# The expert layer of a two-block network on one core: unsplit weight planes, pinned row work, gates with tokens innermost

## The chip, the cores and the metric

The kernel runs on one core of one Trainium2 chip, in one launch. The metric is the device time in microseconds (us). TensorE is PE in the profile, VectorE is DVE, ScalarE is ACT, GpSimd is POOL, and SP only issues transfers.

## The reference, cut to what matters

Two transformer blocks run over 256 tokens of width 1024 in float32. The change lies in the last layer of the first block, an expert layer. Each token picks 16 of 16,384 experts in each of 8 heads, 128 in all:

```
q  = (xc @ w_query);  sc = q . sub_keys            # scores of 2 x 128 keys per head
top 16 of each half -> 256 sums -> top 16          # experts, with softmax gates
u  = expert_down[experts];  vv = expert_up[experts]  # rows of 1024
act = gelu(x . u);  w = gates * act
out = sum over 128 picks of w * vv
```

The second block, the attention of the first and the final normalisation are not touched.

## The kernel before, in words

**Two ways through the experts.** The first 64 tokens (`NS`) are done by fetching: 64 indirect transfers bring 128 rows of `down_rows` each (one per partition, 4 KB a row), and 64 more bring rows of `peer_up`. Partitions 0 to 63 hold one half of a token's picks, partitions 64 to 127 the other half. `fetch` (L733) issues one on the POOL queue into a ring of four buffers (`fetched`, L598); `dot` (L739) multiplies the rows with the token (`rows`, L602 to L604) and sums, one DVE instruction of 128x1024; `axpy` (L839) adds the weighted row of `peer_up` to `sums`, also one DVE instruction of 128x1024.

The other 192 tokens (`ND`) are done densely. **Stage 1** (L795 to L822) computes all 128 planes of 128 experts: a plane is a weight tile of 128x1024 float32, loaded by SP, and eight matmuls (one per slice of 128 columns) multiply it with the 192 tokens. Planes go in pairs, 64 pairs. The first of a pair is split: `stream` (L71) loads it, ACT casts it to a rounded part `hi` (L61), DVE makes the rest `lo` (L62), and `split_plane` (L776) multiplies `hi` with both parts of the tokens at once (384 columns) and `lo` with the rounded tokens (192 columns). The result is in two parts; ACT copies one (L811), DVE adds them (L812). The second plane of a pair is not split: `whole_plane` (L787) multiplies the float32 tile with float32 tokens `xf`. The trace shows such a float32 matmul as two records. ACT then takes the gelu of both planes into `slots` (L816), the SBUF array [128, 128 planes, 192 tokens].

**Gates.** `gates_of` (L745) builds the gates of four tokens as a one-hot matmul: four DVE instructions of 128x512, four ACT instructions, eight small matmuls into a PSUM bank (L767), and then the gates are multiplied into the planes that are finished (L772, DVE) and copied into the slots of those that are not (L774, ACT); a later plane finds its gate there, and DVE multiplies after the gelu (L818, L819). There are 48 such groups, spread between planes `J0` = 48 and `J1` = 120. L772 walks over planes innermost, so neighbouring elements in `slots` are 192 floats apart.

**Selection.** Ahead of stage 1, 16 query groups (L621 to L637) give the scores; DVE then finds the top lists of both halves of the tokens (L648 to L728), in part while stage 1 already runs, in memory that belongs to high planes of `slots`.

**Stage 2** (L862 to L882) runs over 128 `j`: `peer_up[j]` is split as above (L61, L62), the 192 columns of `slots[:, j]` are split into `a2` (L875 on ACT, L876 and L877 on DVE), and ten matmuls of 512 columns accumulate into four PSUM banks.

**Order.** A planner orders each engine's instructions by its own estimate of when each is ready, so the position in the code is a priority and not a place. `tc.keep_in_program_order` puts an instruction behind the one written just before it on its engine. In the kernel before, `dot` and `axpy` are free to move; the code places the dots between pairs 16 and 60 and the axpys over 112 of the 128 `j`. Each engine works in its own order. PSUM has four banks `mm` for planes and two banks `at` for gates.

Of the kernel before, what the change touches and what calls it, by code (L numbers as in the profile page):

```python
# [40 lines left out]
def layers_kernel(ctx: ExitStack, tc: tile.TileContext, a: dict, out: bass.AP, upto: str = "all"):  # L41
# [518 lines left out]
    with ExitStack() as c2:  # L560
        pr = c2.enter_context(tc.tile_pool(name="peer", bufs=1))
        prs = c2.enter_context(tc.tile_pool(name="peers", bufs=2))
        xhl = fx.tile([P, KT, 2, T], F32R, name="fhl")
# [181 lines left out]
        def gates_of(g, j):  # L745
# [27 lines left out]
            if j < P:
                S.copy(sv[:, :, j:], gv[:, :, j:])  # L774

        def split_plane(o, w):  # L776

            for k in range(KT):
                hi, lo = w[0][:, k * P:(k + 1) * P], w[1][:, k * P:(k + 1) * P]
                o2 = o[:, :2 * ND].rearrange("p (s t) -> p s t", s=2)  # L780
                if k < KT - 1:
                    PE.matmul(o2, hi, xhl[:, k, :, NS:], start=(k == 0), stop=False)  # L782
                PE.matmul(o[:, :ND], lo, xhl[:, k, 0, NS:], start=False, stop=False)  # L783
                if k == KT - 1:
                    PE.matmul(o2, hi, xhl[:, k, :, NS:], start=False, stop=True)
# [49 lines left out]
        S.activation(acts, acts, AF.Gelu)  # L835
        V.tensor_tensor(acts, acts, gate_s, op=OP.mult)
        sums = pr.tile([P, D], F32, name="sums", tag="rows_s")

        def axpy(k):  # L839
            r = fetch("peer_up", k)  # L840
            if k == 0:
                V.tensor_scalar(sums, r, acts[:, 0:1], None, op0=OP.mult)
            else:
                V.scalar_tensor_tensor(sums, r, acts[:, k:k + 1], sums, op0=OP.mult, op1=OP.add)  # L844
# [15 lines left out]
        state["k"] = 0  # L860
        K1 = 112
        for j in range(P):  # L862
            while state["k"] < min(HALF, -(-HALF * (j + 2) // K1)):
                axpy(state["k"])
                state["k"] += 1
                if state["k"] == HALF:

                    other = fetched()
                    S.copy(other[:NS], sums[NS:])
                    V.tensor_tensor(x_sb[:NS, 0, :], x_sb[:NS, 0, :], sums[:NS], op=OP.add)  # L870
                    V.tensor_tensor(x_sb[:NS, 0, :], x_sb[:NS, 0, :], other[:NS], op=OP.add)
# [484 lines left out]
```

## Time and profile before

| what | us |
|---|---|
| median of 3 runs | 1521.5 (1518.92 to 1528.25) |
| the profiled execution | 1522.0, span 1520.2 |
| PE busy, share of span | 1425.7, 94% |
| DVE busy | 1098.0, 72% |
| ACT busy | 787.9, 52% |
| POOL busy | 275.6, 18% |

The span is what the profiler saw from the first to the last instruction. [...] The stretches named below are us from the start of the span: the query groups run to about 225, stage 1 from 225 to 632, stage 2 from 632 to about 968, and the second block follows.

### The profile page before, as it was taken

To read this page: it belongs to the slowest core of one execution; us is meant where nothing else is said; L and a number is where in the kernel's file an instruction comes from. 1 tells how busy PE (TensorE), PEld (TensorE's weight loads), DVE (VectorE), ACT (ScalarE), POOL (GpSimd) and SP (SyncE) were. 2 spreads that over 40 slices of the span, in tenths; PEclk is the share of its full clock that TensorE was granted. 3 is DMA by queue.
4 is the path that set the end of the run, shared out by engine and by line. 5 is a ranking of instruction groups with operands and counts; after the bars stand their busy time and mean duration, and the time that the engine had idled before them with its cause. 6 is when DMAs were issued, how large, how long until landed. Compare 5 with 4: busy or idle time off the path is not lost. (4 is left out here: it accounts for less than half of the span.)

```text
span 1520.2 us, 23927 instructions
## 1 busy us (share of the span) xinstructions
PE 1425.7 (94%) x8728; PEld 1261.6 (83%) x8728; DVE 1098.0 (72%) x2133; ACT 787.9 (52%) x1440; POOL 275.6 (18%) x223
## 2 busy tenths in 40 slices
PE   9999995989988889877999999899999999999998
PEld 7778895989988878755888788798799988899886
DVE  7976479987999999878766666646285555566653
ACT  6475453443665555333555555557444545565542
POOL 4711100054333334543000000012001110000000
PEclk9999997999999999989999999999999999999999
DMA  7444653699999888988777776744255664466653
GB/s 272 139 153 153 211 166 125 192 361 380 341 341 316 299 297 286 336 305 297 229 227 223 224 229 226 245 154 153 95 169 173 190 193 153 127 197 192 192 189 116
DMA packets 93702, 336.92 MB, mean 222 GB/s; under 512 B 10736, under 2 KB 12656, under 8 KB 92816
## 3 DMA queue, kind: packets, MB, share of 16 engines
q1 hardware_dynamic: 73376, 259.79, 51.8%
q0 software_dynamic: 19344, 73.41, 13.7%
q10 hardware_dynamic: 864, 2.19, 0.4%
q8 instruction: 69, 1.13, 0.3%
q14 instruction: 49, 0.40, 0.1%
HBM read 331.15 MB, written 4.19 MB: 221 GB/s over the span
## 5 line engine op out<-in xcount | busy, mean ns | idle before, releaser
L62 DVE TENSOR_TENSOR lo<-raw,hi 128x1024 fp32r<-128x1024 f32 x420 | 517.7, 1235 | 296.9 <-ACT hi L61 295.7
L61 ACT CAST hi<-raw 128x1024 fp32r<-128x1024 f32 x420 | 440.5, 1050 | 436.4 <-PE mm L89 115.1
L88 PE MATMUL mm<-rows_h,hi 128*128 128x256 f32 x736 | 204.2, 283 | 2.6 <-ACT qT_x L1194 1.1
L90 PE MATMUL mm<-rows_h,lo 128*128 128x256 f32 x736 | 204.7, 280 | 1.0 <-DVE lo L62 1.0
L89 PE MATMUL mm<-rows_l,hi 128*128 128x256 f32 x736 | 205.0, 280 | 0.0
L789 PE MATMUL mm<-ff,raw_w 128*128 128x192 f32 x1024 | 184.2, 334 | 11.7 <-DVE mm L812 5.0
L789 PEld LDWEIGHTS mm<-ff,raw_w 128*128 128x128 f32 x1024 | 171.3, 194 | 15.4 <-DVE mm L812 6.1
L782 PE MATMUL mm<-fhl,hi 128*128 128x384 f32 x448 | 142.7, 379 | 20.0 <-DVE mm L812 18.6
L88 PEld LDWEIGHTS mm<-rows_h,hi 128*128 128x128 f32 x736 | 137.4, 189 | 4.4 <-ACT hi L61 1.4
L90 PEld LDWEIGHTS mm<-rows_h,lo 128*128 128x128 f32 x736 | 138.6, 189 | 1.6 <-DVE lo L62 1.6
L89 PEld LDWEIGHTS mm<-rows_l,hi 128*128 128x128 f32 x736 | 138.7, 189 | 0.6
L783 PE MATMUL mm<-fhl,lo 128*128 128x192 f32 x512 | 120.6, 256 | 0.0
L735 POOL DMA_INDIRECT fetched<-in_down_rows,picks x64 | 78.2, 1222 | 230.4 <-DVE picks L713 119.9
L853 PE MATMUL mm<-hi,a 128*128 128x512 f32 x256 | 101.7, 405 | 15.8 <-ACT hi L61 7.5
L735 POOL DMA_INDIRECT fetched<-in_peer_up,picks x64 | 90.5, 1414 | 125.0 <-DVE sums L844 74.9
L854 PE MATMUL mm<-lo,a 128*128 128x512 f32 x256 | 101.5, 405 | 5.9 <-DVE lo L62 5.9
L782 PEld LDWEIGHTS mm<-fhl,hi 128*128 128x128 f32 x448 | 85.2, 190 | 22.6 <-issue 15.8
L857 PE MATMUL mm<-lo,a 128*128 128x512 f32 x256 | 102.6, 405 | 0.0
L856 PE MATMUL mm<-hi,a 128*128 128x512 f32 x256 | 100.0, 403 | 0.7 <-ACT a L875 0.7
L783 PEld LDWEIGHTS mm<-fhl,lo 128*128 128x128 f32 x512 | 97.4, 192 | 0.0
L844 DVE SCALAR_TENSOR_TENSOR sums<-fetched,acts,sums 128x1024 f32<-128x1024 f32 x63 | 81.4, 1292 | 10.9 <-DMA fetched<-in_peer_up,picks 10.8
L858 PE MATMUL mm<-hi,a 128*128 128x512 f32 x256 | 85.1, 405 | 0.0
(384 smaller groups left out, 2830.3 us busy)
## 6 DMA issues: line engine op xcount, KB each, us to landing
raw<-in_peer_up SPq DMA_DIRECT2D x128, 512.0 KB
raw_w<-in_peer_down SPq DMA_DIRECT2D x64, 512.0 KB
raw<-in_peer_down SPq DMA_DIRECT2D x64, 512.0 KB
raw<-in_w_in_2t SPq DMA_DIRECT2D x52, 512.0 KB
raw<-in_w_up SPq DMA_DIRECT2D x32, 512.0 KB
raw<-in_w_down SPq DMA_DIRECT2D x32, 512.0 KB
raw<-in_w_in SPq DMA_DIRECT2D x24, 512.0 KB
raw<-in_peer_query SPq DMA_DIRECT2D x16, 512.0 KB
```

The source lines that it names most:

```text
L61: S.copy(hi, src)
L62: V.tensor_tensor(lo, src, f32v(hi), op=OP.subtract)
L88: PE.matmul(o, hi, xh[:, k, :], start=(k == 0), stop=False)
L89: PE.matmul(o, hi, xl[:, k, :], start=False, stop=False)
L90: PE.matmul(o, lo, xh[:, k, :], start=False, stop=(k == kts - 1))
L735: G.indirect_dma_start(out=r, out_offset=None, in_=tables[table], in_offset=bass.IndirectOffsetOnAxis(ap=picks[:, k:k + 1], axis=0))
L782: PE.matmul(o2, hi, xhl[:, k, :, NS:], start=(k == 0), stop=False)
L783: PE.matmul(o[:, :ND], lo, xhl[:, k, 0, NS:], start=False, stop=False)
L789: PE.matmul(o, w[:, k * P:(k + 1) * P], xf[:, k, :], start=(k == 0), stop=(k == KT - 1))
L853: PE.matmul(acc[0][hf], a2[:, 0:P], uh[:, ds], start=first, stop=False)
L854: PE.matmul(acc[0][hf], a2[:, 0:P], ul[:, ds], start=False, stop=last)
L857: PE.matmul(acc[1][hf], a2[:, P:2 * P], ul[:, ds], start=False, stop=False)
```

## The change

Stage 1 loads every plane by the new `stream_whole` and multiplies it by `whole_plane`; `split_plane` and the joining of two parts go, and a pair needs one PSUM bank instead of two. `stream_whole` takes its buffers in turn from the three rings of `raw`, `hi` and `lo`, nine in all. `dot` and `axpy` are pinned in program order and become steps of one list of 128: 92 (`KD`) of them, all 64 dots and 28 axpys, are spread over pairs 12 to 63 of stage 1, the other 36 axpys over the first 112 `j` of stage 2. The ring of fetched rows has five buffers. The gates start at plane 34 and end at 122, and L772 and L774 walk with the four tokens of a group innermost, so that PSUM is read with steps of 128 floats and `slots` in runs of four. The load of the gain and the making of `rows` move from ahead of the query groups to behind them. In `a2` the two DVE subtractions become one of 192 columns and ACT gets a second copy of 64.

```
--- before.py
+++ after.py
@@ -81,6 +81,16 @@
         with tc.high_priority():
             split(raw, hi, lo)
         return hi, lo
+    whole = {"at": 0}
+    def stream_whole(src):
+        tag = ("raw", "hi", "lo")[whole["at"] % 3]
+        whole["at"] += 1
+        w = stream_p.tile([P, CH], F32, name="whole", tag=tag, bufs=3)
+        nc.sync.dma_start(w, src)
+        return w
     def gemm_t(o, xh, xl, w, kts=KT):
         for k in range(kts):
...
@@ -595,13 +605,8 @@
 
         def fetched():
-            return pr.tile([P, D], F32, name="fetched", tag="fetched", bufs=4)
-        grow = fetched()
-        nc.scalar.dma_start(grow, bass.AP(tensor=a["ffn_gain"].tensor, offset=0, ap=[[0, P], [1, D]]))
-        rows = pr.tile([P, D], F32, name="rows_s", tag="rows_s")
-        V.scalar_tensor_tensor(rows[:NS], x_sb[:NS, 0, :], rs_peer[0][:NS], grow[:NS], op0=OP.mult, op1=OP.mult)
-        S.copy(rows[NS:], rows[:NS])
+            return pr.tile([P, D], F32, name="fetched", tag="fetched", bufs=5)
         picks = pr.tile([P, HALF], U32, name="picks")
         gate_s = pr.tile([P, HALF], F32, name="gate_s")
         acts = pr.tile([P, HALF], F32, name="acts")
@@ -636,6 +641,11 @@
             for t in range(NT):
                 S.copy(sc[t][:, hq * 4:hq * 4 + 4, :].rearrange("p a b -> p (a b)"), pss[t])
+        grow = fetched()
+        nc.scalar.dma_start(grow, bass.AP(tensor=a["ffn_gain"].tensor, offset=0, ap=[[0, P], [1, D]]))
+        rows = pr.tile([P, D], F32, name="rows_s", tag="rows_s")
+        V.scalar_tensor_tensor(rows[:NS], x_sb[:NS, 0, :], rs_peer[0][:NS], grow[:NS], op0=OP.mult, op1=OP.mult)
+        S.copy(rows[NS:], rows[:NS])
         tc.keep_in_program_order(V.tensor_copy(iota, iota_f[:, :, None].to_broadcast([P, P, 2])))
         BIG = -3.0e38
@@ -738,7 +748,36 @@
         def dot(k):
             r = fetch("down_rows", k)
-            V.scalar_tensor_tensor(r, r, 1.0, rows, op0=OP.mult, op1=OP.mult, accum_out=acts[:, k:k + 1])
+            tc.keep_in_program_order(V.scalar_tensor_tensor(r, r, 1.0, rows, op0=OP.mult, op1=OP.mult,
+                                                            accum_out=acts[:, k:k + 1]))
+        sums = pr.tile([P, D], F32, name="sums")
+        def axpy(k):
+            r = fetch("peer_up", k)
+            if k == 0:
+                d = V.tensor_scalar(sums, r, acts[:, 0:1], None, op0=OP.mult)
+            else:
+                d = V.scalar_tensor_tensor(sums, r, acts[:, k:k + 1], sums, op0=OP.mult, op1=OP.add)
+            tc.keep_in_program_order(d)
+            if k == HALF - 1:
+                other = fetched()
+                S.copy(other[:NS], sums[NS:])
+                V.tensor_tensor(x_sb[:NS, 0, :], x_sb[:NS, 0, :], sums[:NS], op=OP.add)
+                V.tensor_tensor(x_sb[:NS, 0, :], x_sb[:NS, 0, :], other[:NS], op=OP.add)
+        def step():
+            k = state["k"]
+            state["k"] += 1
+            if k < HALF:
+                dot(k)
+            else:
+                if k == HALF:
+                    S.activation(acts, acts, AF.Gelu)
+                    V.tensor_tensor(acts, acts, gate_s, op=OP.mult)
+                axpy(k - HALF)
         state = {"g": G0, "k": 0}
@@ -766,50 +805,33 @@
                 for i in range(2):
                     PE.matmul(ps[:, k * P:(k + 1) * P], oh1[:, k // 2, :, k % 2], og[i][:, k // 2, :, k % 2],
                               start=(i == 0), stop=(i == 1))
-            gv = ps.rearrange("p (t j) -> p t j", t=TG)
-            sv = slots[:, :, cs].rearrange("p j t -> p t j")
+            gv = ps.rearrange("p (t j) -> p j t", t=TG)
+            sv = slots[:, :, cs]
             if j > 0:
-                V.tensor_tensor(sv[:, :, :j], gv[:, :, :j], sv[:, :, :j], op=OP.mult)
+                V.tensor_tensor(sv[:, :j], gv[:, :j], sv[:, :j], op=OP.mult)
             if j < P:
-                S.copy(sv[:, :, j:], gv[:, :, j:])
-        def split_plane(o, w):
...
         def whole_plane(o, w):
             for k in range(KT):
                 PE.matmul(o, w[:, k * P:(k + 1) * P], xf[:, k, :], start=(k == 0), stop=(k == KT - 1))
-        J0 = 48
-        J1 = 120
-        K0 = 16
-        K1 = 60
+        J0 = 34
+        J1 = 122
+        K0 = 12
+        KD = 92
         for jp in range(P // 2):
             j = 2 * jp
             if j >= J0:
                 while state["g"] < min(NG, G0 - (-(NG - G0) * (j - J0 + 2) // (J1 - J0))):
                     gates_of(state["g"], j)
                     state["g"] += 1
-            while state["k"] < min(HALF, HALF * (jp - K0 + 1) // (K1 - K0)):
-                dot(state["k"])
-                state["k"] += 1
+            while state["k"] < KD * (jp - K0 + 1) // (P // 2 - K0):
+                step()
             nt = state["g"] * TG - NS
-            o1, o = mm_tile(), mm_tile()
-            split_plane(o1, stream(a["peer_down"][j]))
-            raw = pr.tile([P, CH], F32, name="raw_w", tag="raw_w", bufs=2)
-            nc.sync.dma_start(raw, a["peer_down"][j + 1])
-            whole_plane(o[:, ND:2 * ND], raw)
-            part = prs.tile([P, ND], F32, name="part", tag="og0")
-            S.copy(part, o1[:, ND:2 * ND])
-            V.tensor_tensor(o[:, :ND], o1[:, :ND], part, op=OP.add)
+            o = mm_tile()
+            for jj in range(2):
+                whole_plane(o[:, jj * ND:(jj + 1) * ND], stream_whole(a["peer_down"][j + jj]))
             ov = o[:, :2 * ND].rearrange("p (j t) -> p j t", j=2)
             dst = slots[:, j:j + 2, :]
             if nt < ND:
@@ -832,64 +854,46 @@
         acc = [[mm_tile() for _ in range(2)] for _ in range(NT)]
         held = []
...
         def ups(j, w, t):
             uh, ul, a2 = w
+            both, high, low = a2[:, ND:ND + P], a2[:, NS:ND], a2[:, T + NS:]
             first, last = (j == 0), (j == P - 1)
             for hf in range(2):
                 ds = slice(hf * 512, (hf + 1) * 512)
                 if t == 0:
-                    PE.matmul(acc[0][hf], a2[:, 0:P], uh[:, ds], start=first, stop=False)
-                    PE.matmul(acc[0][hf], a2[:, 0:P], ul[:, ds], start=False, stop=last)
+                    PE.matmul(acc[0][hf], both, uh[:, ds], start=first, stop=False)
+                    PE.matmul(acc[0][hf], both, ul[:, ds], start=False, stop=last)
                 else:
-                    PE.matmul(acc[1][hf], a2[:, P:2 * P], uh[:, ds], start=first, stop=False)
-                    PE.matmul(acc[1][hf], a2[:, P:2 * P], ul[:, ds], start=False, stop=False)
-                    PE.matmul(acc[1][hf], a2[:, 2 * P:], uh[:, ds], start=False, stop=last)
-        K1 = 112
+        KU = 112
         for j in range(P):
...
+            while state["k"] < min(2 * HALF, KD + -(-(2 * HALF - KD) * (j + 1) // KU)):
+                step()
             uh, ul = stream(a["peer_up"][j])
-            a2 = prs.tile([P, 6 * NS], F32R, name="a2", tag="oh1")
-            S.copy(a2[:, NS:4 * NS], slots[:, j, :])
-            V.tensor_tensor(a2[:, :NS], slots[:, j, :NS], f32v(a2[:, NS:2 * NS]), op=OP.subtract)
-            V.tensor_tensor(a2[:, 4 * NS:], slots[:, j, NS:], f32v(a2[:, 2 * NS:4 * NS]), op=OP.subtract)
+            a2 = prs.tile([P, 7 * NS], F32R, name="a2", tag="oh1")
+            S.copy(a2[:, :ND], slots[:, j, :])
+            S.copy(a2[:, ND:T], slots[:, j, :NS])
+            V.tensor_tensor(a2[:, T:], slots[:, j, :], f32v(a2[:, :ND]), op=OP.subtract)
...
```

## Rows read from the trace of the kernel before

**Rows 1.** Windows: start:end, length, PE, PEld, DVE, ACT, POOL busy, PEclk, DMA
```profile
225.00:240.00 15.00, 15.00 (x104) 15.00 (x103) 11.77 (x50) 8.10 (x13) 0.00 (x0) 1.00 0.57 182
240.00:270.00 30.00, 14.44 (x85) 14.17 (x84) 30.00 (x191) 7.14 (x13) 0.00 (x0) 0.72 0.27 90
270.00:300.00 30.00, 29.36 (x193) 29.04 (x193) 30.00 (x120) 10.45 (x18) 0.00 (x0) 1.00 0.65 206
300.00:345.00 45.00, 38.74 (x243) 37.10 (x243) 38.59 (x73) 20.74 (x45) 23.98 (x17) 0.98 0.96 354
345.00:372.00 27.00, 25.05 (x162) 24.82 (x161) 17.78 (x31) 8.79 (x15) 12.94 (x10) 0.96 0.98 367
372.00:470.00 98.00, 89.78 (x670) 86.66 (x667) 97.53 (x203) 62.02 (x159) 33.51 (x31) 1.00 0.95 342
470.00:570.00 100.00, 86.54 (x616) 81.32 (x616) 100.00 (x181) 58.61 (x157) 35.51 (x28) 0.98 0.88 303
570.00:632.00 62.00, 56.85 (x392) 54.39 (x392) 59.67 (x92) 28.75 (x75) 28.53 (x18) 0.97 0.85 295
632.00:720.00 88.00, 65.84 (x229) 48.25 (x230) 70.61 (x99) 30.39 (x46) 35.48 (x28) 0.86 0.87 316
720.00:920.00 200.00, 200.00 (x858) 160.60 (x857) 135.74 (x258) 112.90 (x172) 0.00 (x0) 1.00 0.72 226
```

**Rows 2.** Timeline of PE in stage 1: start, us, line, operation, count, [idle]
```profile
233.43 2.76 PE L789 MATMUL mm<-ff,raw_w 128*128 128x192 f32 x16
235.89 0.47 PE L782 MATMUL mm<-fhl,hi 128*128 128x384 f32 x1
238.30 2.76 PE L789 MATMUL mm<-ff,raw_w 128*128 128x192 f32 x16
...
457.56 0.63 PE L767 MATMUL at<-og,oh 128*128 128x128 f16 x8 [1.31 <-DVE oh L760]
458.03 2.81 PE L789 MATMUL mm<-ff,raw_w 128*128 128x192 f32 x16
```

**Rows 3.** Waits between 225 and 300: engine, line, releaser: total us, times, longest
```profile
PE mm L782 <- DVE mm L812: 16.2, 2, 15.6
```

**Rows 4.** Lines of DVE, 225 to 632: count, busy us, mean ns, idle
```profile
L62 DVE TENSOR_TENSOR lo<-raw,hi 128x1024 fp32r<-128x1024 f32 x65 | 81.3, 1251 | 8.1 <-ACT hi L61 8.1
L741 DVE SCALAR_TENSOR_TENSOR fetched<-fetched,rows_s 128x1024 f32<-128x1024 f32 x64 | 77.9, 1218 | 7.9 <-DMA fetched<-in_down_rows,picks 7.9
L844 DVE SCALAR_TENSOR_TENSOR sums<-fetched,acts,sums 128x1024 f32<-128x1024 f32 x35 | 45.4, 1298 | 2.3 <-DMA fetched<-in_peer_up,picks 2.3
L812 DVE TENSOR_TENSOR mm<-mm,part 128x192 f32<-128x192 f32 x63 | 24.6, 391 | 2.6 <-issue 2.6
```

**Rows 5.** Lines of DVE by shape, 372 to 632, PSUM times slots
```profile
L772 DVE TENSOR_TENSOR slots<-at,slots 128x456 f32<-128x456 f32 x2 | 2.4, 1218 | 0.0
L772 DVE TENSOR_TENSOR slots<-at,slots 128x192 f32<-128x192 f32 x2 | 1.1, 576 | 0.3 <-ACT slots L816 0.3
L819 DVE TENSOR_TENSOR slots<-mm,slots 128x384 f32<-128x384 f32 x3 | 1.7, 571 | 0.0
```

**Rows 6.** Timelines of DVE and PE in the query groups
```profile
173.44 1.28 DVE L603 SCALAR_TENSOR_TENSOR rows_s<-x_sb,rrow,fetched 64x1024 f32<-64x1024 f32 x1 [4.62 <-DMA fetched<-in_ffn_gain]
...
175.17 0.38 PE L89 MATMUL mm<-fhl,hi 128*128 128x256 f32 x1 [1.98 <-DVE fhl L188]
```

**Rows 7.** Lines of DVE, 632 to 720
```profile
L844 DVE SCALAR_TENSOR_TENSOR sums<-fetched,acts,sums 128x1024 f32<-128x1024 f32 x29 | 37.2, 1283 | 8.5 <-DMA fetched<-in_peer_up,picks 8.4
L62 DVE TENSOR_TENSOR lo<-raw,hi 128x1024 fp32r<-128x1024 f32 x22 | 25.9, 1222 | 4.8 <-ACT hi L61 4.7
```

**Rows 8.** Lines of DVE and ACT, 720 to 968
```profile
L877 DVE TENSOR_TENSOR a<-slots,a 128x128 fp32r<-128x128 f32 x104 | 29.6, 284 | 0.0
L876 DVE TENSOR_TENSOR a<-slots,a 128x64 fp32r<-128x64 f32 x104 | 22.7, 218 | 0.2 <-ACT a L875 0.2
...
L875 ACT CAST a<-slots 128x192 fp32r<-128x192 f32 x104 | 36.1, 347 | 3.3 <-PE mm L858 1.3 <-issue 1.0 <-ACT hi L61 1.0
```

More of the change, by code (lines that the diff above doesn't have):

```diff
@@ L562, in layers_kernel @@
         prs = c2.enter_context(tc.tile_pool(name="peers", bufs=2))
-        xhl = fx.tile([P, KT, 2, T], F32R, name="fhl")
-        xh, xl = xhl[:, :, 0, :], xhl[:, :, 1, :]
+        xh = fx.tile([P, KT, T], F32R, name="fh")
+        xl = fx.tile([P, KT, T], F32R, name="fl")
         xf = pr.tile([P, KT, ND], F32, name="ff")
@@ L768, in gates_of @@
                               start=(i == 0), stop=(i == 1))
-            gv = ps.rearrange("p (t j) -> p t j", t=TG)
-            sv = slots[:, :, cs].rearrange("p j t -> p t j")
+            gv = ps.rearrange("p (t j) -> p j t", t=TG)
+            sv = slots[:, :, cs]
             if j > 0:
-                V.tensor_tensor(sv[:, :, :j], gv[:, :, :j], sv[:, :, :j], op=OP.mult)
+                V.tensor_tensor(sv[:, :j], gv[:, :j], sv[:, :j], op=OP.mult)
             if j < P:
-                S.copy(sv[:, :, j:], gv[:, :, j:])
-        def split_plane(o, w):
[L778 to L785, printed above, removed]
+                S.copy(sv[:, j:], gv[:, j:])
         def whole_plane(o, w):
@@ L833, in layers_kernel @@
         held = []
[L835 to L844, printed above, removed]
         def ups(j, w, t):
             uh, ul, a2 = w
+            both, high, low = a2[:, ND:ND + P], a2[:, NS:ND], a2[:, T + NS:]
             first, last = (j == 0), (j == P - 1)
@@ L852, in ups @@
                 if t == 0:
-                    PE.matmul(acc[0][hf], a2[:, 0:P], uh[:, ds], start=first, stop=False)
-                    PE.matmul(acc[0][hf], a2[:, 0:P], ul[:, ds], start=False, stop=last)
-                else:
-                    PE.matmul(acc[1][hf], a2[:, P:2 * P], uh[:, ds], start=first, stop=False)
-                    PE.matmul(acc[1][hf], a2[:, P:2 * P], ul[:, ds], start=False, stop=False)
-                    PE.matmul(acc[1][hf], a2[:, 2 * P:], uh[:, ds], start=False, stop=last)
-        state["k"] = 0
-        K1 = 112
-        for j in range(P):
[L863 to L871, printed above, removed]
+                    PE.matmul(acc[0][hf], both, uh[:, ds], start=first, stop=False)
+                    PE.matmul(acc[0][hf], both, ul[:, ds], start=False, stop=last)
+                else:
+                    PE.matmul(acc[1][hf], high, uh[:, ds], start=first, stop=False)
+                    PE.matmul(acc[1][hf], high, ul[:, ds], start=False, stop=False)
+                    PE.matmul(acc[1][hf], low, uh[:, ds], start=False, stop=last)
+        KU = 112
+        for j in range(P):
+            while state["k"] < min(2 * HALF, KD + -(-(2 * HALF - KD) * (j + 1) // KU)):
+                step()
             uh, ul = stream(a["peer_up"][j])
-            a2 = prs.tile([P, 6 * NS], F32R, name="a2", tag="oh1")
-            S.copy(a2[:, NS:4 * NS], slots[:, j, :])
-            V.tensor_tensor(a2[:, :NS], slots[:, j, :NS], f32v(a2[:, NS:2 * NS]), op=OP.subtract)
-            V.tensor_tensor(a2[:, 4 * NS:], slots[:, j, NS:], f32v(a2[:, 2 * NS:4 * NS]), op=OP.subtract)
+            a2 = prs.tile([P, 7 * NS], F32R, name="a2", tag="oh1")
+            S.copy(a2[:, :ND], slots[:, j, :])
+            S.copy(a2[:, ND:T], slots[:, j, :NS])
+            V.tensor_tensor(a2[:, T:], slots[:, j, :], f32v(a2[:, :ND]), op=OP.subtract)
             if j >= P - LASTN:
@@ L882, in layers_kernel @@
                     ups(j, (uh, ul, a2), t)
-        lows = fetched()
+        moved = fetched()
         for t in range(NT):
@@ L889, in layers_kernel @@
                 if t == 0:
-                    S.copy(lows[NS:, ds], acc[0][hf][:NS])
+                    S.copy(moved[NS:, ds], acc[0][hf][:NS])
                     V.tensor_tensor(x_sb[NS:, 0, ds], acc[0][hf][NS:], x_sb[NS:, 0, ds], op=OP.add)
-                    V.tensor_tensor(x_sb[NS:, 0, ds], lows[NS:, ds], x_sb[NS:, 0, ds], op=OP.add)
+                    V.tensor_tensor(x_sb[NS:, 0, ds], moved[NS:, ds], x_sb[NS:, 0, ds], op=OP.add)
                 else:
```

## The prediction

> **What bounds the kernel now.** I read the windows by stretch first, because the change touches two stages only. In stage 1 (225 to 632) PE is never full for long, while DVE is: 30.00 of 30.00 us twice, then 97.53 of 98.00 and 100.00 of 100.00 [rows 1]. [...] So stage 1 is bound by DVE, first by the selection, later by the sum of splits, gates and row work. Stage 2 is two stages in one: from 632 to 720 PE is busy for 65.84 of 88.00 us and DMA moves 316 GB/s at a share of 0.87; from 720 on PE has 200.00 of 200.00 us [rows 1]. The lines of DVE say what is special in the first part: 29 of the 63 adding axpys, beside only 22 splits [rows 7]. The planner let them run as early as they could, although the code spreads them.
>
> **What PE needs.** The pitch comes from starts, not from busy time. A whole plane starts at 233.43 and the split plane behind it at 235.89: 2.46 us. That one takes until 238.30: 2.41 us. A gate group takes 458.03 - 457.56 = 0.47 us [rows 2]. Before, stage 1 needs of PE 64 x (2.46 + 2.41) + 48 x 0.47 = 334 us; it takes 632 - 225 = 407 [rows 1]. So 73 us are waits and low clock. After, it needs 128 x 2.46 + 48 x 0.47 = 337 us: **on PE itself the change costs 3 us**, and what it can gain is the 73.
>
> **What DVE loses and gets.** Its busy time in stage 1, summed over the eight windows, is 385 us [rows 1]. Out go the splits (65 records, 81.3 us) and L812 (63 records, 24.6 us). Row work was 64 dots and 34 adding axpys and the first axpy, some 99; 92 remain, 7 less of 1.3 us, 9 us [rows 4]. That leaves 385 - 81 - 25 - 9 = 270 us in a stage of at least 337. Up to pair 16 no gate exists, so DVE stands nowhere between PE and the gelu, and the 15.6 us stop has no cause left. ACT loses 64 casts and 64 copies and was not full (58.61 of 100 us) [rows 1].
>
> L772 walks differently. Its time rises from 576 ns for 192 elements to 1218 for 456, that is 2.4 ns an element, or 1.04 us at 384; L819, with PSUM and `slots` both in runs, takes 571 ns for 384 [rows 5]. The new walk has runs of four in `slots` but steps in PSUM. Bounds: 0.47 us less for each of 48 (23 us less on DVE) if the stride in `slots` was the price; as much more if the stride in PSUM costs the same. I take 0 on the path: 270 + 23 still lies under 337. [...]
>
> **What the transfers must carry.** A plane and a fetch are both 128x1024 float32 [rows 4], 0.524 MB. In pairs 17 to 63 (47 pairs) a pair brings two planes and 92/52 = 1.77 fetches, 1.976 MB, in the 2 x 2.46 + 48 x 0.47/47 = 5.40 us that PE needs: 366 GB/s. The windows give 354 at a share of 0.96, 367 at 0.98, 342 at 0.95, 303 at 0.88, 295 at 0.85 [rows 1]; scaled to a full share these are 344 to 374. So PE and DMA would be full at the same time. Lower bound of the loss: 0, at 374 (5.28 us a pair), with nine plane buffers and five fetch buffers to even it out. Upper bound: 300 to 372, where DMA was at 0.96 to 0.98, shows PE busy for 63.8 of 72 us [rows 1]; 11% of 47 x 5.40 = 254 us is 28 us. At 344 it is 5.74 us, 16 us in all. I take 15, near that. Stage 1 then takes 337 + 15 = 352: **55 us less**, between 42 and 70.
>
> [...]
>
> **Stage 2.** 858 matmuls in 200 us at ten a `j` are 2.33 us a `j`; the first 88 us hold 229, 22.9 `j`, worth 53.4 us at that pace [rows 1]. The bunched axpys thus cost 34.6 us, part of it low clock (0.86). After, 36 axpys are spread over 112 `j`. Per `j` DVE has 1.22 for the split, 0.32 x 1.28 = 0.41 for rows, and one subtraction of 192 in place of 0.284 + 0.218 (between those 0.50 and 0.28; I take 0.35): 1.98 of 2.33 us [rows 7, 8]. ACT has 112.90/200 of 2.33 = 1.32 and a copy of 64, at most the 0.347 of the copy of 192: 1.66 [rows 1, 8]. DMA carries 1.32 x 0.524 MB in 2.33 us, 297 GB/s, under 344. PE stays the bound. The pin puts each axpy on DVE behind the subtraction of the `j` before, which waits for one of two `a2` buffers, so it can't run ahead; queued behind a waiting axpy are the subtraction and the split of this `j`, and PE behind those with the other buffers still full. I subtract 5 us for that (0 to 15): **30 us less**, 20 to 35.
>
> **Rows made later.** L603 waits 4.62 us for the gain on DVE, with the query's transposes queued behind; PE stops for 1.98 us [rows 6]. Behind the query groups, the load (on ACT's queue), L603 (1.28 us) and ACT's copy fall where DVE feeds only the selection and PE has four banks. I take the 1.98: **2 us less**, 0 to 4.6.
>
> **Sum.** The profiled execution took 1522.0 (span 1520.2), the median is 1521.5: they agree. 1522 - 55 - 30 - 2 = **1435**; with all bounds good 1522 - 70 - 35 - 5 = 1412, with all bad 1522 - 42 - 20 - 0 = 1460. The second block is not touched.
>
> **Rivals.**
> - *Transfers never limit* (14 in 100): stage 1 at 337 to 340, 1412 to 1422. For it: 367 GB/s was seen. Against: PE waited beside it.
> - *Transfers become the bound* (13 in 100): fetches and planes together get what 470 to 632 shows, 299 GB/s: 6.61 us a pair, 47 x 1.21 = 57 us lost, stage 1 at 394, total 1522 - 13 - 30 - 2 = 1477. Against: DVE was full there and set the pace, and the DMA share was only 0.85 to 0.88.
> - *The pin doesn't spread the axpys in stage 2* (6 in 100), so the change doesn't do what it says: 36 in a bunch cost 36/29 x 34.6 = 43 us, 8 more than before: 1522 - 55 + 8 - 2 = 1473. Against it is the buffer wait named above.
> - *Slower* (5 in 100): a pinned row instruction waits for its fetch, and gates, multiplications and splits queue behind it on DVE, until the two gate banks and four plane banks are full. Measured waits for fetches are 7.9 + 2.3 + 8.5 = 18.7 us over 128 [rows 4, 7], 0.15 each, for instructions that the planner could move out of the way. Spare are 67 us of DVE in stage 1; with the 87 of the sum, it decides from (67 + 87)/128 = 1.2 us a row. At 1.6 us it would be 205 - 67 = 138 more: 1573. The fifth buffer and a pace of one per 3.1 us speak against it.
>
> **Chances.** The forecast as it stands has 62 in 100. The range 1412 to 1478 holds it, the first rival, and most of the next two; beyond it lies the slower one and worse mixtures, about 1 in 10. About 1%, 15 us, is what a measurement here can tell from no change. Faster by more than that: the first four cases, less a little for mixtures, 0.92; within 0.04; slower 0.04.
>
> **What would show it.** Right: the 240 to 270 stretch at a clock of 1.0; plane starts 2.46 us apart; stage 1 within 337 to 365 us, with DMA at a share over 0.9 and DVE near 270 us busy; axpys at even distances to the end of stage 2's first 112 `j`, and 2.33 to 2.4 us a `j`. Wrong: PE waiting for planes for over 30 us (transfers), DVE idle before row instructions for over 1 us each with PE idle beside it (pins), an L772 well above 1.2 us, or a clock below 0.95 in stage 1, which sixteen float32 matmuls in a row would then have caused.

## The result and the profile after

The changed kernel takes **1475.95 us** (median of four, 1475.67 to 1476.70) against 1522.38 for the kernel before beside it: a ratio of 0.9692 [0.9661, 0.9723]. That is 46 us faster, where 87 were forecast. The profiled span went from 1520.2 to 1474.4 us, 45.8 less. The stages are cut at the first matmul of each:

| us | before | after | forecast for after |
|---|---|---|---|
| up to stage 1 | 225.4 | 226.1 | 2 less |
| stage 1 | 406.7 | 362.6 | 352 |
| stage 2, to the start of its last `j` | 335.3 | 333.7 | 30 less |
| the rest | 552.8 | 552.0 | unchanged |

**Nearly all of the gain is stage 1's (44.1 us), and stage 2 gave 1.6.** The windows of the changed kernel, with the columns of [rows 1]:

```profile
225.00:240.00 15.00, 15.00 (x98) 15.00 (x97) 9.64 (x58) 3.71 (x6) 1.13 (x2) 1.00 1.02 390
240.00:270.00 30.00, 30.00 (x187) 30.00 (x186) 30.00 (x190) 6.30 (x11) 0.00 (x0) 1.00 0.65 214
270.00:300.00 30.00, 27.77 (x164) 27.41 (x163) 28.32 (x119) 8.83 (x23) 6.57 (x5) 0.94 0.65 228
300.00:345.00 45.00, 45.00 (x308) 44.68 (x307) 27.31 (x63) 13.99 (x45) 18.29 (x15) 1.00 0.99 370
345.00:372.00 27.00, 27.00 (x190) 26.68 (x189) 18.18 (x45) 9.19 (x31) 11.48 (x9) 1.00 0.96 353
372.00:420.00 48.00, 48.00 (x346) 47.42 (x344) 34.44 (x84) 20.24 (x68) 17.68 (x14) 1.00 0.95 346
420.00:470.00 50.00, 50.00 (x355) 49.42 (x355) 37.04 (x89) 18.28 (x63) 19.84 (x16) 1.00 0.94 335
470.00:520.00 50.00, 50.00 (x358) 49.42 (x356) 40.04 (x88) 19.57 (x69) 19.24 (x17) 1.00 0.96 346
520.00:570.00 50.00, 50.00 (x354) 49.42 (x353) 35.85 (x60) 15.94 (x59) 13.30 (x15) 1.00 0.95 353
570.00:592.00 22.00, 22.00 (x131) 21.42 (x131) 15.55 (x19) 4.85 (x7) 10.61 (x8) 1.00 0.74 258
592.00:640.00 48.00, 44.66 (x182) 32.67 (x181) 34.69 (x43) 26.39 (x55) 10.07 (x8) 1.00 0.83 286
640.00:720.00 80.00, 73.53 (x303) 55.02 (x302) 55.95 (x70) 43.22 (x91) 12.86 (x10) 1.00 0.81 262
720.00:800.00 80.00, 73.67 (x298) 55.70 (x299) 54.93 (x70) 42.23 (x90) 10.92 (x10) 0.98 0.81 263
800.00:880.00 80.00, 76.17 (x316) 57.61 (x315) 60.39 (x76) 47.06 (x97) 7.91 (x5) 1.00 0.73 238
880.00:923.00 43.00, 43.00 (x186) 34.48 (x185) 25.77 (x35) 25.05 (x50) 0.00 (x0) 1.00 0.72 229
```

In 240 to 270, where PE was busy for 14.44 us at a clock of 0.72 (0.50 in 250 to 260, where PE stood still), it now has 30.00 of 30.00 us at 1.00, although DVE is as full as before. What is left of the stop stands in 270 to 300, at a clock of 0.94: PE's transposes of the selected lists (L732) wait there for DVE's L709.

```profile
276.68 0.33 PE L732 MATMUL tp<-ident,slots 128*128 128x128 f32 x1 [2.23 <-DVE slots L709]
276.84 9.97 PE L817 MATMUL mm<-ff,whole 128*128 128x192 f32 x50
```

From 300 to the end of stage 1 at 588.7 PE is never idle, DVE has slack, and DMA works at a share of 0.94 to 0.99 until 570. DVE's busy time up to 592 sums to 276 us. In stage 2 the picture is the opposite of the one before: the first 88 us used to be poor and the rest full [rows 1], and now PE falls short evenly, 73.5 to 76 of 80 us, until the last adding axpy at 870.5; behind that it is full.

PE's timeline in stage 1 (start, us, engine, line, operation, tiles, shape, count; L817 is the whole plane, 16 records each, L806 a gate group):

```profile
424.18 5.42 PE L817 MATMUL mm<-ff,whole 128*128 128x192 f32 x32
429.43 0.62 PE L806 MATMUL at<-og,oh 128*128 128x128 f16 x8
429.89 5.42 PE L817 MATMUL mm<-ff,whole 128*128 128x192 f32 x32
435.15 0.62 PE L806 MATMUL at<-og,oh 128*128 128x128 f16 x8
```

Two planes take 429.43 - 424.18 = 5.25 us from start to start, 0.164 us a record; the forecast had 4.92. The same 5.25 stands at 332 (332.26 to 337.52) and at 545.

DVE's lines by shape from 372 on (count, busy us, mean ns, idle) show the gates' multiplication with its new walk, at L811:

```profile
L811 DVE TENSOR_TENSOR slots<-at,slots 128x456 f32<-128x456 f32 x1 | 0.6, 626 | 0.0
...
L811 DVE TENSOR_TENSOR slots<-at,slots 128x384 f32<-128x384 f32 x1 | 0.6, 551 | 0.0
```

456 elements took 1218 ns [rows 5] and take 626. All 48 together take 22.4 us, 467 ns in the mean.

Stage 2's waits, from 592 to 923 (engine, line, releaser: us in total, times, longest; L61 and L62 make `hi` and `lo`, L868 is a matmul, L879 the copy of 192 into `a2`, L761 the axpy):

```profile
POOL fetched L745 <- DVE sums L761: 197.3, 30, 10.7
DVE lo L62 <- ACT hi L61: 96.8, 92, 3.6
ACT hi L61 <- PE mm L870: 81.7, 78, 3.2
ACT hi L61 <- DMA raw<-in_peer_up: 61.3, 30, 3.7
PEld mm L868 <- ACT a L879: 24.7, 20, 2.3
PE mm L868 <- ACT a L879: 16.5, 14, 1.9
```

Thirty times ACT's cast stands still for a weight tile on its way, 61.3 us in all. One of these stops in the timeline (POOL's fetch, SP's weight loads, ACT, then PE; the row of SP groups three issues that begin at 653.22):

```profile
652.32 1.68 POOL L745 DMA_INDIRECT fetched<-in_peer_up,picks  x1 [7.94 <-DVE sums L761]
...
653.22 4.72 SPq L75 DMA_DIRECT2D raw<-in_peer_up  x3
...
660.38 1.04 ACT L61 CAST hi<-raw 128x1024 fp32r<-128x1024 f32 x1 [3.66 <-DMA raw<-in_peer_up]
661.33 0.35 ACT L879 CAST a<-slots 128x192 fp32r<-128x192 f32 x1
...
661.73 0.51 PE L868 MATMUL mm<-hi,a 128*128 128x512 f32 x1 [1.83 <-ACT a L879]
```

A fetch goes out at 652.32, a weight load at 653.22 beside it, and that load is there for the cast at 660.4, some 7 us later. ACT waits 3.66 us in order, with the `a2` copy of this `j` behind the cast; PE, which needs both, stops for 1.83 us.

### The profile page after: what moved, and what is told of

The parts are those of the page before. It is cut to its first block, busy times and chain, and to the rows that moved or that the text cites. A ratio compares the mean times of both kernels' runs of the same rounds, so it can differ in the third digit from the quotient of the medians.

```text
span 1474.4 us, 23648 instructions
## 1 busy us (share of the span) xinstructions
PE 1429.4 (97%) x8728; PEld 1265.8 (86%) x8728; DVE 982.8 (67%) x1884; ACT 716.4 (49%) x1448; POOL 265.5 (18%) x223
## 5 line engine op out<-in xcount | busy, mean ns | idle before, releaser
L62 DVE TENSOR_TENSOR lo<-raw,hi 128x1024 fp32r<-128x1024 f32 x356 | 439.4, 1235 | 303.6 <-ACT hi L61 302.5
L61 ACT CAST hi<-raw 128x1024 fp32r<-128x1024 f32 x356 | 373.3, 1049 | 413.8 <-PE mm L99 112.9
L817 PE MATMUL mm<-ff,whole 128*128 128x192 f32 x2048 | 345.3, 328 | 0.0
L817 PEld LDWEIGHTS mm<-ff,whole 128*128 128x128 f32 x2048 | 333.2, 191 | 0.0
L745 POOL DMA_INDIRECT fetched<-in_peer_up,picks x64 | 77.3, 1208 | 274.7 <-DVE sums L761 255.0
L838 ACT ACTIVATE slots<-mm 128x384 f32<-128x384 f32 (+43 forms) x60 | 22.4, 373 | 200.2 <-PE mm L817 200.1
L868 PE MATMUL mm<-hi,a 128*128 128x512 f32 x256 | 103.3, 403 | 16.6 <-ACT a L879 16.5
L745 POOL DMA_INDIRECT fetched<-in_down_rows,picks x64 | 81.5, 1273 | 176.9 <-DVE fetched L751 105.1
L761 DVE SCALAR_TENSOR_TENSOR sums<-fetched,acts,sums 128x1024 f32<-128x1024 f32 x63 | 80.5, 1277 | 0.1
L751 DVE SCALAR_TENSOR_TENSOR fetched<-fetched,rows_s 128x1024 f32<-128x1024 f32 x64 | 75.8, 1216 | 6.3 <-DMA fetched<-in_down_rows,picks 6.3
L868 PEld LDWEIGHTS mm<-hi,a 128*128 128x128 f32 x256 | 48.1, 188 | 35.6 <-ACT a L879 24.7
L865 PEld LDWEIGHTS mm<-hi,a 128*128 128x128 f32 x256 | 48.2, 188 | 27.9 <-ACT a L879 8.1
```

The costliest lines, as they stand in the source:

```text
L61: S.copy(hi, src)
L62: V.tensor_tensor(lo, src, f32v(hi), op=OP.subtract)
L745: G.indirect_dma_start(out=r, out_offset=None, in_=tables[table], in_offset=bass.IndirectOffsetOnAxis(ap=picks[:, k:k + 1], axis=0))
L817: PE.matmul(o, w[:, k * P:(k + 1) * P], xf[:, k, :], start=(k == 0), stop=(k == KT - 1))
L865: PE.matmul(acc[0][hf], both, uh[:, ds], start=first, stop=False)
L868: PE.matmul(acc[1][hf], high, uh[:, ds], start=first, stop=False)
```

## The experiments

**The theory (A)** for stage 2: three raw buffers are too few for a load that shares the 16 DMA engines with the fetches (61.7% and 16.1% of their time in 640 to 880 of the changed kernel). A buffer is filled again only when the load has landed, ACT has cast it (1.05 us), and DVE has made `lo` from it (1.22 us), which may stand behind an axpy of 1.28. Three buffers at 2.33 us a `j` give 7.0 us for that. From 640 to 880 the loads take 4.6 us to land at the median and 7.1 at most:

```profile
DMA to landing us min/median/max: 3.2/4.6/7.1
```

4.6 + 1.05 + 1.22 = 6.9, nothing to spare. In the expectations below A still names the landing alone; that DVE's part of the trip belongs to it came with s2_short. The rivals: the rate of the transfers as such, DVE's time as such, or the two `a2` tiles (C). The first four kernels tell these apart, the others take the change to pieces. Each is compared with the kernel before beside it; stage times are from the traces.

| kernel | median us | ratio | stage 1 | stage 2 |
|---|---|---|---|---|
| changed kernel | 1475.95 | 0.9692 [0.9661, 0.9723] | 362.6 | 333.7 |
| s2_none | 1450.14 | 0.9542 [0.9526, 0.9558] | 363 | 303.2 |
| s2_nofetch | 1451.78 | 0.9547 [0.9528, 0.9566] | 363 | 303.3 |
| s2_short | 1456.68 | 0.9599 [0.9571, 0.9628] | 363 | 312.5 |
| s2_raw5 | 1444.97 | 0.9509 [0.9493, 0.9524] | 362 | 302.5 |
| before_raw5 | 1506.32 | 0.9891 [0.9855, 0.9926] | 406 | 319 |
| unsplit_only | 1463.54 | 0.9608 [0.9582, 0.9634] | 365 | 318.9 |
| alt_split | 1487.92 | 0.9780 [0.9750, 0.9811] | 369 | 332.7 |
| walk_only | 1503.91 | 0.9884 [0.9850, 0.9918] | 389 | 334.3 |
| gates_old | 1475.68 | 0.9688 [0.9654, 0.9722] | 363 | 333.5 |
| pins_off | 1472.50 | 0.9666 [0.9636, 0.9697] | 370 | 321.4 |
| pins_off_raw5 | 1457.20 | 0.9580 [0.9545, 0.9616] | 368 | 307.8 |
| mix_raw5 | 1441.71 | 0.9466 [0.9445, 0.9488] | 355 | 305.8 |

### s2_none: stage 2 without the row work

The kernel leaves out 35 of the 36 axpys of stage 2, with their fetches.

```diff
-            while state["k"] < min(2 * HALF, KD + -(-(2 * HALF - KD) * (j + 1) // KU)):
-                step()
+            if j == 0:
+                state["k"] = 2 * HALF - 1
+                step()
```

> The changed kernel without 35 of the 36 axpys that it places in stage 2 (neither fetch nor DVE instruction; they are left out of the sum). Theory A, transfers: beside a fetch a weight tile of stage 2 lands later than its ring of three raw buffers allows, ACT's cast waits for it and the a2 copy stands behind that cast; without fetches stage 2 runs at 2.33 us a j, 298 us instead of 334, total 1476 - 35 = 1441. Theory B, DVE: the 1.28 us of a pinned axpy delay lo and the subtraction; also 1441. Theory C, the a2 copies (ACT now has two, and they stand behind the cast of the next tile): nothing to do with rows, total stays at 1470 to 1476.

Stage 2 takes 303.2 us, 30.5 less, with PE full (its windows, columns as above):

```profile
640.00:720.00 80.00, 80.00 (x344) 64.14 (x343) 51.28 (x70) 49.66 (x103) 0.00 (x0) 1.00 0.70 226
```

The loads land after 3.5 us at the median, 4.6 at most. So the paced rows cost the changed kernel 30.5 us, about what the bunch cost before (335.3 - 303.2 = 32). The total missed the expected 1441 by 9 us. Stage 2 is 5 of them (298 were expected), and the rest is not the second block's: the last transfer of the output is issued 548.4 us behind the start of the last `j` here and 548.5 in s2_raw5, but the span then runs on for 8.3 us instead of 3.4. In s2_nofetch these are 549.8 and 8.6. Why the span ends later in these two is not shown.

### s2_nofetch: the axpys stay on DVE, their fetches go

```diff
-            r = fetch("peer_up", k)
+            r = fetch("peer_up", k) if k < KD - HALF else rows
```

> The changed kernel with the 36 axpys of stage 2 kept on DVE, but reading a tile that is already there instead of a fetched one, so that 36 transfers of 0.5 MB are left out. Theory A (transfers): total 1441 to 1446, stage 2 about 300 us. Theory B (DVE's 1.28 us): total stays at 1470 to 1476. Theory C: stays.

```profile
640.00:720.00 80.00, 80.00 (x344) 63.30 (x343) 62.75 (x81) 49.87 (x103) 0.00 (x0) 1.00 0.70 226
```

Stage 2 takes 303.3 us, and the total misses its 1441 to 1446 as in s2_none. DVE carries every axpy (62.75 of 80 us, more than in the changed kernel) and PE is full. DVE's time is not the price by itself. The loads land after 4.1 us, and ACT waits 7.8 us for them in 640 to 860.

### s2_short: the fetches stay, the axpys touch 16 of 1024 columns

```diff
-                d = V.scalar_tensor_tensor(sums, r, acts[:, k:k + 1], sums, op0=OP.mult, op1=OP.add)
+                n = D if k < KD - HALF else 16
+                d = V.scalar_tensor_tensor(sums[:, :n], r[:, :n], acts[:, k:k + 1], sums[:, :n], op0=OP.mult, op1=OP.add)
```

> The changed kernel with all fetches, but the 36 axpys of stage 2 work on 16 of 1024 columns, so that DVE is busy for about 0.1 us instead of 1.28 each. Theory A (transfers): total stays, 1466 to 1476. Theory B (DVE): total 1441 to 1446. If both count by their size, about 1458.

```profile
640.00:720.00 80.00, 79.18 (x329) 60.59 (x329) 50.62 (x78) 47.74 (x99) 11.18 (x11) 1.00 0.87 286
```

Stage 2 takes 312.5 us: 21 come back although every fetch is there. That is a miss for A as expected (1466 to 1476) and for B (1441 to 1446); 1456.68 lies at the third case, both by their size (about 1458). The short axpys take 0.23 us each ((42.8 - 27 x 1.28)/36, from the line of all 63 adding ones), where the expectation estimated 0.1. The waits of the cast for its load are 32.0 us in 640 to 860, against 45.3 in the changed kernel and none in s2_none. Neither half alone is the price: taking the transfers away returns 30, taking DVE's time away 21. 30 and 21 together are more than the 30.5 us there are, so they can't be two separate prices; they draw on one common slack, which is A with DVE's part in the buffers' round trip.

### s2_raw5: the whole kernel, with five raw buffers in stage 2

Two tiles that nothing reads any more in stage 2 join the ring of three (the token rows of the dots, and the tokens in float32).

```diff
-        raw = stream_p.tile([P, CH], F32, name="raw", tag="raw", bufs=3)
+        if raws["pool"] is not None and raws["at"] % (3 + len(raws["tags"])) >= 3:
+            tag = raws["tags"][raws["at"] % (3 + len(raws["tags"])) - 3]
+            raw = raws["pool"].tile([P, CH], F32, name="raw", tag=tag, bufs=1)
+        else:
+            raw = stream_p.tile([P, CH], F32, name="raw", tag="raw", bufs=3)
+        raws["at"] += 1
...
+        raws.update(pool=pr, at=0, tags=('rows_s', 'ff'))
         for j in range(P):
```

> The changed kernel, complete, with five raw buffers in stage 2 instead of three (two tiles that are free by then, the token rows and the float32 tokens of stage 1, join the ring). Theory A (landing time against a ring of three): ACT no longer waits for raw, stage 2 falls from 334 to 300 to 308 us, total 1442 to 1450. Theory B (DVE) and theory C (a2): total within 5 us of 1476. If transfers are limited by their rate and not by when they are issued, it stays as well.

**This settles it.** Nothing is left out, and stage 2 takes 302.5 us, as without any row work; the kernel takes 1444.97 us. Its windows, then the first three of its waits in 640 to 860 (L877 is the last matmul of a `j`, L768 the axpy), and the landing in 640 to 880:

```profile
640.00:720.00 80.00, 80.00 (x345) 63.51 (x344) 63.37 (x80) 49.60 (x104) 16.06 (x11) 1.00 0.90 298
720.00:800.00 80.00, 80.00 (x345) 63.41 (x344) 63.63 (x80) 49.31 (x103) 19.10 (x12) 1.00 0.88 299
```

```profile
POOL fetched L752 <- DVE sums L768: 123.4, 22, 7.7
ACT hi L61 <- PE mm L877: 82.5, 93, 1.1
DVE lo L62 <- ACT hi L61: 46.8, 65, 1.0
```

```profile
DMA to landing us min/median/max: 3.1/5.2/7.7
```

The loads land later than with three buffers (5.2 us at the median, 7.7 at most), DMA moves more (298 GB/s), DVE is fuller, and none of it reaches PE: the row "ACT hi <- DMA raw" is gone. Five buffers give 11.7 us for a round trip. C falls, since the two `a2` tiles are as they were, and so do the rate of the transfers and DVE's time as prices of their own.

### before_raw5: the deeper ring in the kernel before

The same edit in the kernel before, whose free tiles there are `raw_w` (two) and `ff`.

```diff
+        raws.update(pool=pr, at=0, tags=('raw_w', 'ff'))
         for j in range(P):
```

> The kernel before with a deeper ring of raw buffers in stage 2 alone (two tiles that are free by then join the three). If the ring of three, and not the bunch of axpys as such, cost stage 2 its 35 us: stage 2 falls from 335 to 303 to 315 us, total 1490 to 1502. If the bunched fetches starve the planes by their rate, whatever the ring: 1515 to 1522.

A miss by half. Stage 2 takes 319 us, 16 less than in the kernel before, where A alone would have returned about 30.

```profile
640.00:720.00 80.00, 74.57 (x299) 55.88 (x299) 69.59 (x111) 38.05 (x59) 38.72 (x22) 0.98 0.97 362
```

In the bunch DMA is at a share of 0.97 and DVE at 69.59 of 80 us. So about half of the bunch's cost was the shallow ring, and the other half goes with the bunch. With five buffers spreading removes that half too (302.5 us); with three it gained nothing (333.7).

### unsplit_only: the kernel before, with whole planes alone

`stream_whole` is added as in the change.

```diff
-            split_plane(o1, stream(a["peer_down"][j]))
-            raw = pr.tile([P, CH], F32, name="raw_w", tag="raw_w", bufs=2)
...
-            V.tensor_tensor(o[:, :ND], o1[:, :ND], part, op=OP.add)
+            o = mm_tile()
+            for jj in range(2):
+                whole_plane(o[:, jj * ND:(jj + 1) * ND], stream_whole(a["peer_down"][j + jj]))
```

> The kernel before with the unsplit planes alone (nine plane buffers; no pins, dots and axpys where they were, gates with planes innermost, rows ahead of the query groups, four fetch buffers). If the planes are the whole gain: stage 1 at 363 to 370 us, total 1476 or less; with axpys that the planner now fits into stage 1, as low as 1445. If pins and gates are needed for it: 1490 or more.

One part of the change alone gives a ratio of 0.9608, below that of the whole change. Stage 1 takes 365 us, 41 of the 44. Stage 2 takes 318.9: the planner again runs the axpys early, only 25 of the 63 adding ones behind stage 1, and the last starts at 647. From 720 on PE is full:

```profile
590.00:640.00 50.00, 41.58 (x163) 28.86 (x161) 47.00 (x67) 20.64 (x32) 33.03 (x21) 1.00 0.96 362
...
720.00:800.00 80.00, 80.00 (x345) 64.45 (x344) 53.23 (x103) 44.91 (x69) 0.00 (x0) 1.00 0.71 225
```

### alt_split: the changed kernel, with its first planes split again

```diff
-            o = mm_tile()
-            for jj in range(2):
-                whole_plane(o[:, jj * ND:(jj + 1) * ND], stream_whole(a["peer_down"][j + jj]))
+            o1, o = mm_tile(), mm_tile()
+            split_plane(o1, stream(a["peer_down"][j]))
+            whole_plane(o[:, ND:2 * ND], stream_whole(a["peer_down"][j + 1]))
...
+            V.tensor_tensor(o[:, :ND], o1[:, :ND], part, op=OP.add)
```

> The changed kernel with only the unsplit planes undone: the first plane of each pair is split again, pins, spreading, gates and moved rows stay. Theory A: unsplit planes paid because they free DVE (split and joining, about 1.6 us a pair, 104 us in all), while on TensorE they cost 0.35 us a pair (a float32 matmul of 192 columns takes two records of 0.164 us, 2.62 us a plane; the split plane has a pitch of 0.285 us, 2.28). Then TensorE would need 22 us less here, but DVE gets 276 + 104 = 380 us in stage 1 and binds: stage 1 takes 380 to 405 us instead of 363, total 1493 to 1520. Theory B: the gain came from pins and gates, and the planes are neutral or bad: stage 1 at 340 to 365, total 1455 to 1478.

Between the two theories, and a miss for both: stage 1 takes 369 us.

```profile
225.00:300.00 75.00, 55.20 (x353) 54.32 (x352) 70.72 (x355) 24.42 (x44) 0.07 (x1) 0.89 0.44 154
300.00:372.00 72.00, 71.72 (x508) 70.83 (x506) 66.93 (x143) 42.94 (x103) 35.59 (x25) 1.00 0.96 361
372.00:590.00 218.00, 213.73 (x1572) 208.57 (x1571) 212.31 (x423) 126.18 (x351) 96.11 (x67) 1.00 0.95 350
```

The stop behind the selection is back: PE has 55.20 of 75 us at 0.89. Behind 300, though, DVE carries the splits (212.31 of 218 us) and PE still has 98%. The cheap walk alone gives 18 of these 38 us (walk_only, below), and seven adding axpys fewer fall into stage 1 (28 instead of 35); what else of pins, spreading and gates makes up the other 20 was not taken apart. Unsplit planes alone give 41 us, everything else without them 38, both together 44. I read this as two ways to relieve DVE, behind which PE is the bound.

### walk_only and gates_old: the walk of the gates alone, and everything else

```diff
-            gv = ps.rearrange("p (t j) -> p t j", t=TG)
-            sv = slots[:, :, cs].rearrange("p j t -> p t j")
+            gv = ps.rearrange("p (t j) -> p j t", t=TG)
+            sv = slots[:, :, cs]
...
```

This goes into the kernel before as walk_only, and is undone in the changed kernel as gates_old.

> The kernel before with the new walk of the gates alone (L772 and L774 with tokens innermost). In the changed kernel the multiplication takes 470 ns on the mean, in the kernel before 890: 48 x 0.42 = 20 us of DVE. Theory A: stage 1 before was bound by DVE (100 of 100 us busy), so it gives most of that: stage 1 387 to 392 us, total 1502 to 1508. Theory B: the selection's stop and the clock set the loss and the walk is hidden: 1518 to 1522.

> The changed kernel with the old walk of the gates alone. DVE gets 20 us more in stage 1, where it is busy for about 276 of 363 us and TensorE is full: under both theories that leave TensorE the bound, total 1474 to 1480. If DVE's order counts (pinned rows stand behind the multiplication), 1485 or more.

Where DVE is the bound, the walk is worth 18 us of stage 1 (407 to 389) and 1.2% of the time; the 48 multiplications fall from 43.1 to 23.2 us. Where PE is the bound it is worth nothing: with the old walk they take 39.8 us, with the new one 22.4 (the lines of gates_old and of the changed kernel, 225 to 1000), DVE works 175 us instead of 161 in 372 to 590, and stage 1 stays at 363.

```profile
L811 DVE TENSOR_TENSOR slots<-at,slots 128x136 f32<-128x136 f32 (+43 forms) x48 | 39.8, 830 | 3.7 <-PE at L806 3.7
L811 DVE TENSOR_TENSOR slots<-at,slots 128x136 f32<-128x136 f32 (+43 forms) x48 | 22.4, 467 | 4.8 <-PE at L806 4.8
```

The 470 and 890 ns of the expectation are medians over groups of different lengths; like for like the walk saves 0.41 us a group in the kernel before and 0.36 in the changed one.

### pins_off and pins_off_raw5: row instructions without the pin, with three and with five raw buffers

```diff
-            tc.keep_in_program_order(V.scalar_tensor_tensor(r, r, 1.0, rows, op0=OP.mult, op1=OP.mult,
-                                                            accum_out=acts[:, k:k + 1]))
+            V.scalar_tensor_tensor(r, r, 1.0, rows, op0=OP.mult, op1=OP.mult, accum_out=acts[:, k:k + 1])
...
-            tc.keep_in_program_order(d)
```

> The changed kernel without the two pins: the planner places dots and axpys itself. If the pins carried the gain (bunched axpys cost stage 2 35 us before): total 1500 or more. If the freed DVE carries it: rows run early, stage 1 stays at 363 to 370 us since TensorE is full there, all or nearly all axpys fall into stage 1, and stage 2 goes down towards 303 us: total 1445 to 1465, that is, the pin that holds 36 axpys back to stage 2 costs time.

> The changed kernel without the two pins and with five raw buffers in stage 2. If the pins and the spreading are needed once the ring is deep enough: 1455 or more against 1445 with them. If a deep ring hides bunched axpys as well: stage 1 at 370 us (as without pins before), stage 2 at 303 to 306, total 1448 to 1454. If the pins cost by themselves: under 1445.

With three buffers the pins are worth nothing that can be measured (0.9666 against 0.9692, the intervals overlap): without them stage 1 is 7 us longer and stage 2 is 12 shorter, its last axpy at 645. Neither expected range (1500 or more, 1445 to 1465) holds 1472.50. With five they are worth 12 us (1457.2 against 1445.0, the intervals are apart). The unpinned kernel then pays in stage 1 (368 against 362) and for 23 axpys bunched at the start of stage 2, at a DMA share above 1:

```profile
590.00:640.00 50.00, 48.76 (x208) 37.09 (x207) 49.11 (x57) 25.75 (x53) 33.94 (x20) 1.00 1.02 404
```

So spreading paid, but only beside a ring that can bear it.

### mix_raw5: five raw buffers, and 24 of the 64 pairs split again

```diff
+            if jp >= 16 and jp % 2 == 0:
+                o1, o = mm_tile(), mm_tile()
+                split_plane(o1, stream(a["peer_down"][j]))
+                whole_plane(o[:, ND:2 * ND], stream_whole(a["peer_down"][j + 1]))
```

> The complete kernel with five raw buffers in stage 2, and in stage 1 the first plane of every other pair from pair 16 on split again (24 of 64). Theory A (a split plane is 0.35 us cheaper on TensorE, and DVE has about 77 us to spare from 300 us on, of which 24 x 1.6 = 39 are used): stage 1 takes 363 - 8 = 355 us, total 1445 - 8 = 1437. If whole and split planes cost the same on TensorE, as the prediction had it: 1445. If DVE or the shared plane buffers can't keep up: 1447 or more.

With PE the bound and DVE at three quarters (161 of 218 us in 372 to 590 of s2_raw5), the quicker split pairs may come back where no selection stands on DVE. Stage 1 is 7 us shorter than in s2_raw5 (8 were expected) and stage 2 3 longer, for a reason that no run shows:

```profile
372.00:590.00 218.00, 216.45 (x1538) 212.32 (x1536) 192.67 (x378) 104.23 (x306) 95.53 (x72) 1.00 0.96 362
```

At 1441.71 us (1441.30 to 1442.66) it is the fastest kernel here, 5.3% under the kernel before and 2.3% under the changed one.

## Why the prediction was half right

**What held.** The bound of stage 1 was DVE, and the change took it off PE's path: the stop at L812 (15.6 us [rows 3]; L812 runs at 260.89, behind lines of the selection, L655 to L704) is gone and the clock in 240 to 270 is 1.00. That "the 15.6 us stop has no cause left" was too much: a stop of 2.23 us remained, at the transposes behind the selection, with a clock of 0.94 in 270 to 300. That is below the 0.95 named as a sign of being wrong, but the float32 matmuls weren't the cause: they ran at 1.00 in the windows on either side (240 to 270 and 300 to 345). DVE's busy time is 276 us where 270 were worked out, in part by luck: the 270 leave out what the walk saves, some 20 us, and they take whole durations off the busy time, though durations overlap on DVE (its lines in stage 1 before sum to 476 us, its busy time to 385). The walk came out near its good end, 0.36 us less for each of 48 where 0.47 was the bound, and hidden, as I took it. Here a strided read of PSUM had no price on DVE: 551 ns for 384 elements stand beside the 571 of L819, which reads runs [rows 5]. The pin spread the axpys (505.6 to 870.5 us), and the slower rival did not come: the pinned row instructions waited 6.3 us for fetches in all of stage 1.

**The step that failed** is in stage 2: "I subtract 5 us for that (0 to 15): **30 us less**, 20 to 35". The paced rows cost 30.5 us and the stage gained 1.6. I had each engine's load per `j` (DVE 1.98, ACT 1.66 of 2.33 us) and the rate of the transfers (297 GB/s), and none of them was too low: s2_raw5 shows PE full at 1.85 us of DVE, 1.44 of ACT and 298 GB/s. What I did not add up is the round trip of a raw buffer, against three pitches. The queue that I named, behind a waiting axpy on DVE, is only one part of that trip. The wait fell elsewhere: on ACT, where the cast waits for its load and the `a2` copy stands behind it. My 297 GB/s "under 344" looked only at the mean, while the stop above comes from one load that took 7 us instead of 3.5.

**The terms that were mis-sized** in stage 1 nearly cancel, and that the stage came out within 11 us of its forecast is luck to that extent. "On PE itself the change costs 3 us": it costs 24. I took 2.46 us for a whole plane from a start to the first start of another kind of matmul; inside a run the records stand 0.164 us apart, 2.62 a plane. A pair took 4.87 us before (233.43 to 238.30 [rows 2]) and takes 5.25: 64 x 0.38 = 24 us, and 64 x 5.25 + 48 x 0.46 = 358 is nearly all of the stage's 362.6. "I take 15, near that", for the transfers: it is 0, for PE is full from 300 on at the same 5.25 us that it shows at 545. A pair with its fetches then wants 1.976 MB in 5.25 + 0.46 = 5.71 us, 346 GB/s, and the windows from 300 to 570 show 335 to 370; the most in a window shown here is 404 GB/s, at a share of 1.02 (pins_off_raw5), and PE asks for less than that in stage 1. Stage 1 was thus forecast at 337 + 15 and is 358 + 5. The rival that transfers never limit was right in its mechanism and wrong in its time, by PE's 21 us.

**Rows made later** brought 0 and not 2 us. The lines moved in the code, but not on the chip: the load carries no pin, and the planner put it back among the query's transposes. DVE's timeline:

```profile
169.93 0.48 DVE L198 SCALAR_TENSOR_TENSOR fl<-tp,gcols,fh 128x256 fp32r<-128x256 f32 x1 [1.19 <-ACT fh L197]
175.32 1.28 DVE L647 SCALAR_TENSOR_TENSOR rows_s<-x_sb,rrow,fetched 64x1024 f32<-64x1024 f32 x1 [4.91 <-DMA fetched<-in_ffn_gain]
176.52 0.28 DVE L649 CAST iota<-slots 128x256 bf16<-128x256 f32 x1
176.72 0.86 DVE L198 SCALAR_TENSOR_TENSOR fl<-tp,gcols,fh 128x256 fp32r<-128x256 f32 x2
```

L647 waits 4.91 us with the transposes' work (L198) behind it, as L603 waited 4.62 [rows 6].

**What stays open:** why the span ends some 5 us later behind the last output transfer in s2_none and s2_nofetch; how the bunch's other half in before_raw5 is divided between the transfers and DVE; and whether four buffers, or the `a2` copy ahead of the cast on ACT, would have done in stage 2 as well.

## What to carry to other kernels

Before transfers are spread beside a weight stream, set the ring against its round trip: buffers times pitch against the landing time under that load (its late ones, not the median), plus the cast, the remainder and what stands ahead of them in order. Here 7.0 us against 7.1 + 1.05 + 1.22 cost 30 us, and 11.7 against 7.7 + 1.05 + 1.22 cost none; the mean rate and each engine's load can all be fine while this is not. Take an instruction's pitch from inside a run of its own kind, never from its start to the start of another kind (2.62 against 2.46 us here). When two edits relieve the same engine, expect little more than the larger of their gains (41 and 38 us gave 44 here), and look at what the next bound costs; and a line moved in the code without a pin may not have moved.
